# Loading sixteen tiles of a rotary-embedding kernel in 13 transfers in place of 9

## The chip, the cores and the metric

The kernel runs on one core of a Trainium2 chip. The metric is the device time of one execution, in microseconds (us). Kernels that are compared ran in the same rounds on the same chip; a run counts as slow, and stays out of the ratios, when it is over 1.5% above the fastest of its kernel, and all others count as fast. The profile's span (84.2 us) is some 1.8 us shorter than the device time (86.0), since it counts from the program's first to its last recorded instruction.

## The reference

A rotary position embedding in float32, where the last dimension of 64 is split in halves:

```python
# x: (8, 8, 1024, 64); cos_cached, sin_cached: (1024, 32)
out_first  = x_first * cos_cached - x_second * sin_cached
out_second = x_first * sin_cached + x_second * cos_cached
out = concatenate([out_first, out_second], axis=-1)
```

It reads 16.8 MB of x and writes as much, and does only four multiplications and two additions or subtractions for each pair of elements.

## The kernel before

x is cut into 16 tiles of 128 partitions x 2048 numbers (1 MB, 8 KB for each partition). Each tile has its own place on the chip, so no load waits for a store. SyncE issues all loads, the first two tiles singly and the rest in pairs:

```python
xt = []
for first, n in [(0, 1), (1, 1)] + [(c, 2) for c in range(2, n_ch, 2)]:
    t = xp.tile([P, n, F], fp32, name=f"x{first}")
    nc.sync.dma_start(out=t, in_=xf[first:first + n].rearrange("c p m -> p c m"))
    xt += [t[:, i] for i in range(n)]
```

The arithmetic is divided in four ways. Each tile needs two products (with sine and with cosine) and two sums of half size. The scratch tiles `vs` come from a pool of six.

```python
def vector_pool(c, cuts=(0, R)):        # products on VectorE, sums on GpSimd
    s = tv.tile([P, F], fp32, name="vs")             # pool tv: bufs=6
    products(nc.vector, c, s, csp, snp)
    for n0, n1 in zip(cuts, cuts[1:]):
        sums(nc.gpsimd, c, s, n0, n1)
        store(nc.sync, c, n0, n1)
# vector_tensor(c): products on VectorE, sums on TensorE, stored by ScalarE's queue
# on_pool(c):       all on GpSimd, stored by SyncE
def vector_alone(c):                    # all on VectorE
    products(nc.vector, c, acc, csp, snp)
    sums(nc.vector, c, acc, 0, R)
    store(nc.scalar, c)

vector_tensor(0); on_pool(1); vector_pool(2); vector_pool(3); vector_tensor(4)
on_pool(6); vector_pool(5); vector_tensor(7); vector_pool(8); vector_tensor(9)
vector_pool(10); vector_tensor(11); vector_pool(12); vector_pool(13)
vector_pool(14, (0, G, R)); vector_alone(15)
```

SyncE's transfers go through queue q1 and ScalarE's through q10. In the built program the transfers use eight semaphores in turn, so that the issue of a transfer may have to wait until the one eight places before it has landed.

## Time and profile before

| | before |
|---|---|
| device time, median (range) of the first 3 runs | 85.98 us (85.84 to 86.1) |
| span of the profiled run | 84.2 us |
| moved in the span | 33.82 MB, mean 402 GB/s |
| VectorE (DVE) busy | 70.4 us, 84% |
| GpSimd (POOL) busy | 71.4 us, 85% |
| TensorE (PE) / ScalarE (ACT) busy | 40.1 us / 15.7 us |

Two engines are at some 85%, but the DMA engines, read slice by slice, are at nine tenths or more nearly from start to end; the prediction shows those lines. The page's last part tells the two forms of load apart. Its columns are: what is written from what, the issuing queue, the operation and how many, the size of each, and the median time from issue to landing.

```profile
x<-in_x_dram SPq DMA_DIRECT2D x7, 2048.0 KB, 25.0
...
x<-in_x_dram SPq DMA_DIRECT2D x2, 1024.0 KB, 6.3
```

A pair took 25 us from issue to landing although its data alone need 5 us: all loads are issued early and stand in a queue. A long time to landing in this part is a queue, not a slow transfer.

### The profile page before, as it was taken

The page shows a single profiled execution, that of the slowest core. Times are in us where ns is not written, and L with a number is a line of the kernel's source. Part 1 is how long each engine was busy: PE and PEld are TensorE (multiplying, and loading weights), DVE is VectorE, ACT ScalarE, POOL GpSimd, SP SyncE. Part 2 cuts the span into 40 slices and gives each one's busy share as a digit, 9 for nine tenths or more (in the row PEclk, how much of TensorE's full clock was granted, in tenths as well). Part 3 has the DMA queues.
Part 4 walks back from the last instruction along what each step waited for, and adds up shares of the span by engine and source line. Part 5 has one row for each costly group of instructions (what it writes and reads, how often), then busy time and mean ns, then how long its engine had stood idle before and what let it go on. Part 6 is the DMA issues. An engine that isn't in the chain of part 4 may idle for free.

```text
span 84.2 us, 363 instructions
## 1 busy us (share of the span) xinstructions
PE 40.1 (48%) x80; PEld 15.7 (19%) x80; DVE 70.4 (84%) x34; ACT 15.7 (19%) x16; POOL 71.4 (85%) x38
## 2 busy tenths in 40 slices
PE   0000005994930896895949497794949600000000
PEld 0000002422400341423314051332414100000000
DVE  0199997999999999999999982999999999996000
ACT  4399000004040003104040402204040310000000
POOL 3199999999999999999999999999999999970000
PEclk9999999999999569999999999999999999555555
DMA  3899999999999999999999999999999999999991
GB/s 29 282 432 409 420 420 436 417 409 420 436 428 409 417 428 432 432 424 409 421 436 436 432 421 417 424 424 436 432 432 432 413 421 428 428 436 407 432 419 55
DMA packets 4736, 33.82 MB, mean 402 GB/s; under 512 B 448, under 2 KB 448, under 8 KB 768
## 3 DMA queue, kind: packets, MB, share of 16 engines
q1 hardware_dynamic: 3824, 27.40, 78.7%
q10 hardware_dynamic: 912, 6.42, 18.1%
HBM read 17.04 MB, written 16.78 MB: 402 GB/s over the span
## 4 chain that ended last, share of the span: by engine, by line
POOL 53%; DVE 23%; issue 9%; DMA 4%; DVEq 1%; POOLq 0%
POOL x L94 13%; POOL x L93 11%; DVE vs L88 11%; POOL x L89 11%; POOL gs L88 11%; DVE x L89 8%; POOL sn L77 4%; DMA sn<-in_sin_cached_dram 4%; POOL cs L77 3%; DVE acc L88 3%; DVE x L93 1%; DVEq L170 1%; POOLq L93 0%; POOLq L77 0%
## 5 line engine op out<-in xcount | busy, mean ns | idle before, releaser
L119 PE MATMUL acc<-x,plus 128*128 128x512 f32 x40 | 23.3, 666 | 26.4 <-DVE x L89 13.6
L89 DVE TENSOR_TENSOR x<-x,csp 128x2048 f32<-128x2048 f32 x14 | 32.0, 2287 | 0.6
L88 DVE TENSOR_TENSOR vs<-x,snp 128x2048 f32<-128x2048 f32 x13 | 29.7, 2282 | 2.2 <-POOL x L94 1.7
L122 ACT COPY x<-acc 128x1024 f32<-128x1024 f32 x10 | 10.1, 1012 | 49.2 <-PE acc L120 49.2
L94 POOL TENSOR_TENSOR x<-x,vs 128x1024 f32<-128x1024 f32 (+1 forms) x9 | 19.0, 2108 | 0.0
L93 POOL TENSOR_TENSOR x<-x,vs 128x1024 f32<-128x1024 f32 (+1 forms) x9 | 18.9, 2105 | 0.0
L119 PEld LDWEIGHTS acc<-x,plus 128*128 128x128 f32 x40 | 7.5, 208 | 39.4 <-issue 23.9
L120 PE MATMUL acc<-vs,minus 128*128 128x512 f32 x20 | 11.6, 666 | 0.0
L120 PE MATMUL acc<-vs,plus 128*128 128x512 f32 x20 | 10.2, 592 | 0.0
L89 POOL TENSOR_TENSOR x<-x,cs 128x2048 f32<-128x2048 f32 x2 | 9.1, 4546 | 0.2
L88 POOL TENSOR_TENSOR gs<-x,sn 128x2048 f32<-128x2048 f32 x2 | 9.1, 4542 | 0.1
L73 DVE COPY snp<-sn 32x1024 f32<-32x1024 f32 x4 | 4.9, 1223 | 3.9 <-DMA sn<-in_sin_cached_dram 3.8
L120 PEld LDWEIGHTS acc<-vs,minus 128*128 128x128 f32 x20 | 4.4, 219 | 5.9 <-issue 5.9
L77 POOL COPY sn<-sn 32x1024 f32<-32x1024 f32 x3 | 3.1, 1032 | 2.7 <-DMA sn<-in_sin_cached_dram 2.6
L93 POOL TENSOR_TENSOR x<-x,gs 128x1024 f32<-128x1024 f32 x2 | 4.7, 2362 | 0.2
L94 POOL TENSOR_TENSOR x<-x,gs 128x1024 f32<-128x1024 f32 x2 | 4.7, 2357 | 0.0
L120 PEld LDWEIGHTS acc<-vs,plus 128*128 128x128 f32 x20 | 3.8, 190 | 4.8 <-issue 4.8
L74 ACT COPY csp<-cs 32x1024 f32<-32x1024 f32 x4 | 4.0, 1008 | 1.5 <-DMA cs<-in_cos_cached_dram 1.4
L77 POOL COPY cs<-cs 32x1024 f32<-32x1024 f32 x3 | 3.1, 1033 | 0.1
L88 DVE TENSOR_TENSOR acc<-x,snp 128x2048 f32<-128x2048 f32 x1 | 2.3, 2297 | 0.0
L71 ACT ACT_TABLE_LOAD x1 | 1.3, 1283 | 1.2 <-PEq L159 1.2
L93 DVE TENSOR_TENSOR x<-x,acc 128x1024 f32<-128x1024 f32 x1 | 1.2, 1223 | 0.0
(8 smaller groups left out, 2.4 us busy)
## 6 DMA issues: line engine op xcount, KB each, us to landing
x<-in_x_dram SPq DMA_DIRECT2D x7, 2048.0 KB, 25.0
out_dram<-x SPq DMA_DIRECT2D x9, 1024.0 KB, 13.0
out_dram<-x ACTq DMA_DIRECT2D x6, 1024.0 KB, 9.0
x<-in_x_dram SPq DMA_DIRECT2D x2, 1024.0 KB, 6.3
out_dram<-x SPq DMA_DIRECT2D x2, 512.0 KB, 6.0
cs<-in_cos_cached_dram ACTq DMA_DIRECT2D x1, 128.0 KB, 3.4
sn<-in_sin_cached_dram SPq DMA_DIRECT2D x1, 128.0 KB, 3.1
```

The source lines that it names most:

```text
L71: nc.scalar.mul(minus, plus, -1.0)
L73: nc.vector.tensor_copy(out=snp[r * Q:(r + 1) * Q], in_=sn[0:Q])
L74: nc.scalar.copy(out=csp[r * Q:(r + 1) * Q], in_=cs[0:Q])
L77: nc.gpsimd.tensor_copy(out=t[r * Q:(r + 1) * Q], in_=t[0:Q])
L88: eng.tensor_tensor(out=rows(s), in0=xr, in1=tab(stab), op=TT.mult)
L89: eng.tensor_tensor(out=xr, in0=xr, in1=tab(ctab), op=TT.mult)
L93: eng.tensor_tensor(out=xr[:, :, 0], in0=xr[:, :, 0], in1=sr[:, :, 1], op=TT.subtract)
L94: eng.tensor_tensor(out=xr[:, :, 1], in0=xr[:, :, 1], in1=sr[:, :, 0], op=TT.add)
L119: nc.tensor.matmul(a[:, k], plus, xr[:, :, k], start=True, stop=False)
L120: nc.tensor.matmul(a[:, k], plus if k else minus, sr[:, :, 1 - k], start=False, stop=True)
L122: nc.scalar.copy(out=xr, in_=a.rearrange("p k n j -> p n k j"))
L170: with _tile.TileContext(nc) as tc:
```

## The change

The first ten tiles are loaded one by one and the last six in pairs. The intent is that the first tile of each early pair need not wait for the second, so that the engines get their data up to 2.5 us earlier. It costs four more transfers (32 in place of 28).

```diff
-    for first, n in [(0, 1), (1, 1)] + [(c, 2) for c in range(2, n_ch, 2)]:
+    for first, n in [(c, 1) for c in range(10)] + [(c, 2) for c in range(10, n_ch, 2)]:
```

## The prediction

> **What bounds the kernel now.** I read the page's slices first, because they tell in which stretch which resource is full.
>
> ```profile
> DMA  3899999999999999999999999999999999999991
> GB/s 29 282 432 409 420 420 436 417 409 420 436 428 409 417 428 432 432 424 409 421 436 436 432 421 417 424 424 436 432 432 432 413 421 428 428 436 407 432 419 55
> ...
> HBM read 17.04 MB, written 16.78 MB: 402 GB/s over the span
> ```
>
> Each slice is 84.2 / 40 = 2.1 us. From the third slice to the last but one the DMA engines are at nine tenths or more, with no dip, and the rate stays between 407 and 436 GB/s. To see whether "nine tenths" hides idle time, I then asked for the busy time by stretch (columns: engines, granted clock, DMA share, GB/s).
>
> ```profile
> 15.00:25.00 10.00, 7.73 (x15) 2.68 (x13) 9.93 (x5) 2.02 (x2) 9.88 (x4) 1.00 1.01 421
> 35.00:45.00 10.00, 7.79 (x18) 3.04 (x17) 9.93 (x5) 2.02 (x2) 9.84 (x4) 1.00 1.02 428
> 55.00:65.00 10.00, 7.80 (x18) 3.06 (x17) 9.93 (x5) 2.02 (x2) 9.97 (x5) 1.00 1.02 430
> 75.00:82.00 7.00, 0.00 (x0) 0.00 (x0) 2.19 (x2) 0.00 (x0) 0.30 (x1) 0.50 1.01 423
> 82.00:84.20 2.20, 0.00 (x0) 0.00 (x0) 0.00 (x0) 0.00 (x0) 0.00 (x0) 0.50 0.14 60
> ```
>
> The DMA share is 1.0 in all of them, up to 82. The packet records begin at 1.8 us and end at 82.7, so 33.82 MB take 80.9 us, 418 GB/s on average. VectorE (DVE) and GpSimd (POOL) are nearly as full, so the chain of work that ended last has to be read too (start, length, what).
>
> ```profile
> 0.73 3.08 DMA sn<-in_sin_cached_dram
> ...
> 49.65 2.30 POOL x L94
> 51.95 0.02 issue
> 51.98 2.30 DVE vs L88
> ...
> 74.84 1.22 DVE x L93
> 76.06 1.13 DVEq L170
> ```
>
> It starts at the sine table, not at a tile of x. It goes along GpSimd without a gap until 51.95, passes to VectorE, and ends at 77.2. But the span ends at 84.2. What lies between is told by the DMA view of 77 to 84 us:
>
> ```profile
> q1 hardware_dynamic: 321, 1.19, 41.4%
> q10 hardware_dynamic: 144, 1.05, 35.4%
> ...
> out_dram<-x ACTq DMA_DIRECT2D x1, 1024.0 KB, 5.9
> ```
>
> The last store (tile 15, 1.05 MB on q10) is issued at 77.2 and lands 5.9 us later. In that time the engines also move 1.19 MB of earlier stores from q1, together 2.24 MB; at 423 GB/s that is 5.3 us, hence until about 82.5, and the packets do end at 82.7. So the end is set by the queue of bytes, not by the compute chain. The chain even has room: q1's 1.19 MB are 2.8 us of work, and a transfer needs about 1.0 us to its first packet (the tables are issued at 0.73, the first packet is at 1.8), so the last tile could be some 1.5 us later and the engines would still not run dry (my estimate from these numbers).
>
> **What the Trainium skill says.** "DMA: Bandwidth & Descriptors", section "Issuing engines are not separate DMA queues": transfers from all queues run on the same 16 DMA engines. The trace agrees: q1 and q10 together fill a share of 1.0 and never more. Its section "Where 436 GB/s comes from" puts the ceiling at 435 GB/s; the stretches here, at 421 to 430, are within 4% of it, so little rate is left to win. Its section "Why a DMA increments its semaphore by 16 and not by 1" says that each engine taking part ends a transfer with a write to the semaphore; the page counts 448 packets under 512 B, which is 28 transfers x 16. Its section "Measured (HBM→SBUF, 128 partitions, SWDGE, issued from GpSimd)" gives 341 GB/s for 1 MB and 425 for 16 MB, which would speak against smaller transfers; but that is for transfers one at a time, and here they stand in a queue.
>
> **The change part by part.**
>
> *Removed and added.* Four pair loads (tiles 2 to 9) become eight single ones. No byte and no instruction of the computing engines changes; the built program has the same order on each of them. Four more transfers bring 4 x 16 = 64 more semaphore packets. Such packets last 9.4 ns on average in the trace; 64 x 9.4 ns / 16 engines = 0.04 us of engine time.
>
> *Rate of single loads.* The kernel before has both forms next to each other: tile 1 alone is moved at 6.5 to 9.0, then the pair 2 and 3.
>
> ```profile
> 6.50:9.00 2.50, 0.00 (x0) 0.00 (x0) 2.43 (x3) 1.75 (x2) 2.42 (x3) 1.00 1.01 419
> 9.00:11.50 2.50, 0.00 (x0) 0.00 (x0) 2.40 (x2) 0.00 (x0) 2.37 (x3) 1.00 1.02 426
> ```
>
> By the landings tile 1 took 9.03 - 6.48 = 2.55 us and a pair 4.93 to 4.97. If all of the difference were a cost of a transfer c, then b + c = 2.55 and 2b + c = 4.95, so b = 2.40 and c = 0.15, and four more transfers cost 0.6 us. Against it: from 55 to 65 everything that moves is single stores of 1 MB, and the rate there is the highest, 430 GB/s. I choose a cost near zero, and keep 0.6 us as the upper end.
>
> *Moved: arrivals.* A single tile comes every 2.48 us behind tile 1, so tile 2 lands at about 11.5 in place of 13.96, tile 4 at 16.5 in place of 18.9, and so on; the odd tile of each pair comes when it came before. Who waited for these? In the waits by engine x stands once:
>
> ```profile
> DVE vs L88 <- POOL x L94: 1.7, 1, 1.7
> DVE vs L88 <- DMA x<-in_x_dram: 0.4, 1, 0.4
> ```
>
> VectorE is done with tile 0 at 13.55 and starts tile 2 at 13.99: 0.44 us go. From then on it is busy until 50.2, where it waits 1.74 us for a scratch buffer that GpSimd frees at 51.95. GpSimd's work does not start from an x load (it starts tile 1 at 10.44, after its table copies; tile 1 landed at 9.03), so 51.95 stays. The 0.44 us gained turn into a buffer wait of 1.74 + 0.44 = 2.2 us, and VectorE still ends at 77.2.
>
> *Moved: issues on SyncE.* Semaphores for transfers are handed out in a ring of eight in the built program, so a transfer waits for the one eight before it. With more transfers these pairings shift: loads 12-13 and 14-15 now wait for tiles 5 and 6 to land, at 6.48 + 5 x 2.48 = 18.9 and at 21.4. When load 14-15 is issued, tiles 7 to 13 are still queued, seven times 2.5 us. The first store of SyncE (tile 1) waits for tile 8, about 27 in place of 24.33, tile 2's store for tile 0's store to land (34.0) and tile 3's for load 10-11 (36.2). All are behind the loads in q1, whose last one lands at 48.75, so these delays cost nothing. Tile 6's store now waits for tile 4's store, 48.6 in place of 47.4; tiles 1 to 3 (3 MB, 7 us) are queued by then. No later pairing is later than the computing engine, beyond a microsecond for tile 8.
>
> *Sum.* 85.98 + 0.04 (semaphores) + 0 to 0.6 (single form, taken near 0) - 0 (VectorE, swallowed twice: by the buffer wait and by the DMA queue) = 86.0.
>
> **The rivals.** (a) *Earlier data shortens the time.* If VectorE set the end, 0.44 us could go: 85.5. For it: VectorE is on the chain for its last 25 us. Against it: the wait for GpSimd at 51.95 lies between, and the end is the byte queue's. (b) *Each transfer has a price in the queue.* Then 86.6; for it the 2.55 us of tile 1, against it the rate of the stores. (c) *The shifted waits starve the engines*: a store held back on SyncE also holds all behind it, and if q1 and q10 ran empty, that idle time would be added one for one. To reach 2% it would have to be 1.7 us of all engines. By the reckoning above at least 2 MB, 5 us, stand in the queues at each changed wait. Times: 86.5 to 88. (d) *A better mix*: if reads and writes side by side ran faster than reads alone, earlier stores would help; but reads alone run at 421 to 426 and the mix at 423 to 430, and stores do not come earlier. At best 85.7.
>
> **Range and chances.** Runs of the kernel before span 85.84 to 86.1, and the sum is the same time. Rival (a) or (d) gives the low end, 85.5, rival (b) the high end, 86.6. Only (c) leads out of 2%, and I give it 2 in 100; faster by 2% would need the byte queue to move at 434 GB/s or more on average from the first packet to the last, which I give 1 in 100.
>
> **What would show the steps right or wrong.** Right: 512 packets under 512 B; DMA share 1.0 in all stretches from 5 to 82; the wait of VectorE for an x load gone and its wait for GpSimd at 2.2 us; GpSimd's handover still at about 51.95; VectorE's end at about 77.2; the last store landing at about 83.2. Rival (a) shows as an earlier last packet at the same rate and bytes; (b) as a rate of 411 to 419 GB/s between 9 and 24 us, in place of 423 to 426; (c) as a slice of DMA under 9 in the middle, with a SyncE wait for a transfer ending there. The prediction is wrong if the time leaves 85.5 to 86.6, and its mechanism is wrong if the DMA share falls below 1.0 anywhere before the last store.

## The result

The changed kernel took 86.15 us in the median of six runs (85.91 to 86.24), the kernel before 85.97 us (85.79 to 86.1) in the same rounds. The ratio is 1.0016, with a 95% interval of 0.9996 to 1.0036: the same time. Ratios here are the mean time of one kernel's fast runs over that of the other's fast runs of the same rounds, so they are not quite the ratio of the medians quoted.

The page of the changed kernel, its slices, its count of packets and its loads:

```profile
DMA  0999999999999999999999999999999999999991
GB/s 4 307 420 405 424 436 428 393 424 436 432 409 413 397 432 428 436 416 413 424 436 436 428 432 420 416 420 432 436 436 428 432 405 428 424 436 413 434 434 62
DMA packets 4800, 33.82 MB, mean 402 GB/s; under 512 B 512, under 2 KB 512, under 8 KB 832
...
x<-in_x_dram SPq DMA_DIRECT2D x10, 1024.0 KB, 14.3
...
x<-in_x_dram SPq DMA_DIRECT2D x3, 2048.0 KB, 23.3
```

The bytes and the mean rate are those of before, 33.82 MB and 402 GB/s. There are 512 packets under 512 B, 64 more, 16 for each added transfer. The busy time by stretch has no idle DMA either. Its columns are the stretch and its length in us, the busy us and the number of instructions of PE, of its weight loads, of DVE, ACT and POOL, the granted clock of TensorE, the DMA share and GB/s. (A packet counts whole in the stretch in which it starts, so a share can read a little over 1.0.)

```profile
15.00:25.00 10.00, 8.68 (x15) 3.05 (x14) 9.90 (x6) 1.20 (x2) 9.84 (x5) 1.00 1.02 426
35.00:45.00 10.00, 7.80 (x18) 2.87 (x16) 9.93 (x5) 2.02 (x2) 9.84 (x3) 1.00 1.02 430
75.00:82.00 7.00, 0.00 (x0) 0.00 (x0) 2.21 (x2) 0.00 (x0) 0.25 (x1) 0.50 1.01 423
```

Now the waits of VectorE. Before, it waited 0.4 us for x and 1.7 us for GpSimd. In the waits of the changed kernel one line is left:

```profile
DVE vs L88 <- POOL x L94: 2.2, 1, 2.2
```

VectorE starts tile 2 at 13.55 in place of 13.99, and keeps that lead until 49.8. There it waits 2.20 us for the scratch buffer of tile 5, which GpSimd frees at 51.98 in this run and freed at 51.95 in the one before. The chain of work that ended last shows the handover and the end, hardly moved (start, length, what; DVEq is VectorE's instruction queue):

```profile
49.69 2.29 POOL x L94
51.98 0.02 issue
52.00 2.30 DVE vs L88
...
76.08 1.13 DVEq L170
```

The last store, in the DMA view from 77 to 84 us, again finds 1.25 MB of q1 ahead of it and takes 6.0 us, where it took 5.9:

```profile
q1 hardware_dynamic: 329, 1.25, 43.6%
q10 hardware_dynamic: 144, 1.05, 35.4%
...
out_dram<-x ACTq DMA_DIRECT2D x1, 1024.0 KB, 6.0
```

It landed at 83.24, and at 83.16 before (landings of the trace). The issues of SyncE did move. The store of tile 1 went out at 26.54 in place of 24.33, that of tile 2 at 35.46 in place of 28.93, that of tile 3 at 36.55 in place of 34.11. SyncE's waits say for what; first a line of the kernel before, then one of the changed kernel (in total, times, longest):

```profile
SPq L97 <- DMA x<-in_x_dram: 19.0, 3, 8.1
```

```profile
SPq L97 <- DMA out_dram<-x: 20.6, 3, 9.1
```

SyncE now waits 20.6 us for earlier stores, where it waited 5.6. None of it shows in the time, because q1 was still moving loads until 48.8, and the stores stood behind these anyway.

### The profile page after: what moved, and what is told of

Its sections match the earlier page's. It is cut to its first block, busy times and chain, and to the rows that moved or that the text cites. A ratio compares the mean times of both kernels' runs of the same rounds, so it can differ in the third digit from the quotient of the medians.

```text
span 84.2 us, 367 instructions
## 1 busy us (share of the span) xinstructions
PE 39.5 (47%) x80; PEld 15.3 (18%) x80; DVE 70.3 (84%) x34; ACT 15.7 (19%) x16; POOL 71.2 (85%) x38
## 2 busy tenths in 40 slices
DMA packets 4800, 33.82 MB, mean 402 GB/s; under 512 B 512, under 2 KB 512, under 8 KB 832
## 4 chain that ended last, share of the span: by engine, by line
POOL 49%; DVE 23%; issue 14%; DMA 4%; DVEq 1%; POOLq 0%
POOL x L94 12%; DVE vs L88 11%; POOL x L89 11%; POOL gs L88 11%; POOL x L93 9%; DVE x L89 8%; DMA sn<-in_sin_cached_dram 4%; POOL sn L77 4%; POOL cs L77 3%; DVE acc L88 3%; DVE x L93 1%; DVEq L170 1%; POOLq L93 0%; POOLq L77 0%
## 5 line engine op out<-in xcount | busy, mean ns | idle before, releaser
L120 PE MATMUL acc<-vs,minus 128*128 128x512 f32 x20 | 11.1, 639 | 0.0
```

What stands on the lines that cost most here:

```text
L120: nc.tensor.matmul(a[:, k], plus if k else minus, sr[:, :, 1 - k], start=False, stop=True)
```

## The experiments

Theory 1 is the prediction's: the queue of bytes sets the end, and the 0.44 us that VectorE gains go into waits. Theory 2: the chain of computing engines sets the end, with the last store as a fixed tail. Theory 3: the earlier arrival is worth nothing to begin with. Rivals b and c are the prediction's (a price for each transfer; starved DMA engines). Kernels are compared only within the same rounds. An edit is shown against the changed kernel, unless said otherwise.

### Taking away the wait for the scratch buffer

```diff
-    tv = ctx.enter_context(tc.tile_pool(name="tv", bufs=6))
+    tv = ctx.enter_context(tc.tile_pool(name="tv", bufs=7))
```

> The changed kernel with seven scratch buffers for VectorE in place of six, so that the 2.2 us wait for GpSimd at 52 us goes; bytes and transfers are the same. Theory 1 (the end is set by the queue of bytes): VectorE ends at about 75.0 in place of 77.2, the last store is issued about 2.2 us earlier and lands about 2.2 us later after its issue (8.2 us in place of 6.0), the last landing stays at 83.2, the time within 0.3 us of the kernel before (85.7 to 86.3). Theory 2 (the chain of computing engines sets the end): about 84.0, 2 us less.

Measured: 85.83 us against 85.89 of the kernel before, ratio 0.9993 (0.9981 to 1.0006). The wait of VectorE for GpSimd is gone, and VectorE ended 2.6 us earlier, at 74.6 (0.3 us of it because it began earlier in this run). In the DMA view from 74.3 us on, VectorE's last store took nearly all of that back, and GpSimd's last half store (tile 14) took 8.2 us too:

```profile
out_dram<-x ACTq DMA_DIRECT2D x1, 1024.0 KB, 8.1
out_dram<-x SPq DMA_DIRECT2D x1, 512.0 KB, 8.2
```

The half store landed last here, at 83.08, after VectorE's at 82.72. That it was GpSimd's work that held the end is excluded: the half store was issued at 74.91, and in `less_bytes` below, where the queue is short, it lands 2.6 us after its issue. So even the whole wait, five times the gain of the change, is worth nothing that the interval shows. Theory 2, which expected 84.0, falls.

### Taking bytes away, leaving the arithmetic

```diff
         sums(nc.gpsimd, c, s, 0, R)
-        store(nc.sync, c)                      # tiles 1 and 6
 ...
-            store(nc.sync, c, n0, n1)
+            if c not in (2, 3):
+                store(nc.sync, c, n0, n1)
```

> The changed kernel without the stores of tiles 1, 2, 3 and 6 (4.2 MB less of 33.8; the result is wrong on purpose, those rows are never written); the computing engines do the same work. Theory 1 (byte queue): the DMA engines run dry in between and the last store finds a short queue, so it lands about 4 us after its issue in place of 6.0; VectorE still ends at 77.2; time about 84.1 (83.7 to 84.6), 2 us less. Theory 2 (computing chain, with a fixed cost of 5.9 us for the last store): 86.0.

Measured: 84.05 us, ratio 0.9785 (0.9772 to 0.9798), 1.9 us less. The missing rows make the result wrong. VectorE ended at 77.0, 0.2 us from where it ends in the changed kernel. The DMA engines now have idle time (stretches), and the last store takes 3.9 us:

```profile
50.00:60.00 10.00, 7.19 (x16) 2.88 (x16) 8.13 (x4) 1.99 (x2) 10.00 (x5) 1.00 0.65 269
...
75.00:77.00 2.00, 0.00 (x0) 0.00 (x0) 2.00 (x2) 0.00 (x0) 0.06 (x1) 0.50 0.69 277
```

With the same arithmetic the kernel ends 1.9 us sooner as soon as the queue is shorter. Of the 6.0 us that the last store takes in the changed kernel, 3.9 are its own, and 2.1 are the queue before it. That second number should be the room that the computing chain has; the next two runs test it.

### Making the computing chain longer

Products whose values are written again just after were added before the last tile, half of one (`late_half`) or two full ones (`late_two`, whose edit is shown):

```diff
 def vector_alone(c):
+    for _ in range(2):
+        nc.vector.tensor_tensor(out=rows(acc), in0=rows(xt[c]), in1=tab(snp), op=TT.mult)
     products(nc.vector, c, acc, csp, snp)
```

> The changed kernel with one more half multiply of VectorE (1.2 us, its result is overwritten by the same values) before the last tile, so the last store is issued at about 78.4. Theory 1 with the estimate of 1.5 us of room: time unchanged within 0.3 us (85.8 to 86.4). Theory 2: 1.2 us more, 87.2.

> The changed kernel with two more full multiplies of VectorE (2 x 2.3 = 4.6 us) before the last tile, so the last store is issued at about 81.9. Theory 1 with 1.5 us of room: 4.6 - 1.5 = 3.1 us more, about 89.2 (88.7 to 89.8), and a dip in the DMA share before the last store. Theory 2: 4.6 us more, 90.6.

Measured: `late_half` took 86.01 us, ratio 1.0013 (0.9999 to 1.0026); its last store was issued 1.1 us later (78.37 in place of 77.24) and landed in 4.9 us in place of 6.0. `late_two` took 88.51 us, ratio 1.0301 (1.0287 to 1.0315), 2.6 us more. Its stretches at the end show where the queue ran dry:

```profile
75.00:79.00 4.00, 0.00 (x0) 0.00 (x0) 3.97 (x2) 0.00 (x0) 0.14 (x1) 0.50 1.00 415
79.00:81.00 2.00, 0.00 (x0) 0.00 (x0) 1.97 (x3) 0.00 (x0) 0.00 (x0) 0.50 0.40 162
81.00:83.00 2.00, 0.00 (x0) 0.00 (x0) 0.76 (x1) 0.00 (x0) 0.00 (x0) 0.50 0.23 94
```

Of 4.6 us added, 2.6 came out, so 4.6 - 2.6 = 2.0 us were room. This agrees with the 2.1 us above; the prediction's estimate of 1.5 us was too low, and the expectation of 89.2 (88.7 to 89.8) therefore too high, a miss.

### More and fewer transfers

`all_single` loads all sixteen tiles singly (35 transfers), `fours` loads tiles 4 to 15 in fours (25 transfers):

```diff
-    for first, n in [(c, 1) for c in range(10)] + [(c, 2) for c in range(10, n_ch, 2)]:
+    for first, n in [(c, 1) for c in range(n_ch)]:                                          # all_single
+    for first, n in [(0, 1), (1, 1), (2, 2)] + [(c, 4) for c in range(4, n_ch, 4)]:         # fours
```

> All sixteen tiles loaded one by one, 35 transfers. Theory 1 (a transfer costs its bytes, and 16 semaphore packets of 9.4 ns on 16 engines): 86.0, as before. Rival b (0.15 us for each transfer): 7 more than in the kernel before, 1.05 us more, 87.0. Rival c (the ring of eight holds stores back and the engines run dry): over 86.5 with a dip in the DMA share.

> Tiles 4 to 15 loaded in fours, 25 transfers. Tile 4 then lands at about 23.9 in place of 18.9, and VectorE wants it at 23.0, so about 0.9 us of wait, which the buffer wait at 52 us should swallow (1.74 - 0.9 = 0.8 us left). Theory 1: 86.0. Rival b: 3 transfers less, 0.45 us less, 85.5. Theory 2 with arrivals that matter: up to 0.9 us more, 86.9.

Measured: `all_single` 86.2 us, ratio 1.0014 (0.9998 to 1.003); `fours` 86.01 us, ratio 0.9999 (0.9983 to 1.0015). Both shared their rounds with the same runs of the kernel before, so the ten transfers between them are worth 0.0015 x 86 = 0.13 us, 0.013 us for each, inside the noise (the upper end for `all_single`, 1.003, is 0.26 us for seven transfers more, under 0.04 us for each). The stretch from 9 to 24 us, in which all four kernels move nothing but loads, has the same rate in each; in order, the kernel before, the changed kernel, `all_single` and `fours`:

```profile
9.00:24.00 15.00, 9.08 (x16) 3.52 (x16) 14.38 (x7) 1.14 (x2) 14.71 (x6) 1.00 1.02 425
```

```profile
9.00:24.00 15.00, 9.16 (x15) 3.82 (x16) 14.83 (x7) 1.01 (x1) 14.71 (x6) 1.00 1.01 422
```

```profile
9.00:24.00 15.00, 9.51 (x16) 3.81 (x16) 14.83 (x7) 1.01 (x1) 14.72 (x6) 1.00 1.01 423
```

```profile
9.00:24.00 15.00, 9.22 (x15) 3.86 (x16) 13.59 (x7) 1.01 (x1) 14.71 (x6) 1.00 1.01 421
```

The rates of 421 to 425 GB/s follow no order by the size of a transfer. Rival b's 0.15 us per transfer is excluded (it would be 1.05 us for `all_single`), and the profile of `all_single`, with the most loads, has a DMA share of nine tenths or more in every slice between the first two and the last, so rival c falls too. In `fours` VectorE waited 1.2 us for x, and its wait for GpSimd shrank to 0.8 us: the buffer wait swallows a loss as it swallows a gain.

### Is the gain real at all?

Two pairs of twins, each with the loads of before and with those of the change. The lean twins combine the seven buffers with the missing stores of tiles 1, 2, 3 and 6 (the edits above). `lean_pairs` starts from the kernel before, `lean_singles` from the changed one.

> The kernel before (pair loads) with both swallowers taken away: seven scratch buffers, and no stores of tiles 1, 2, 3 and 6 (wrong result on purpose). VectorE waits 0.44 us for tile 2 and then no more, and ends at about 75.4. Theory 1 (the earlier tile is a true gain that the buffer wait and the byte queue swallow): this one is 0.4 us slower than its twin with single loads; both near 82.3. Theory 3 (single loads bring nothing even there, since the two forms cost the same and the tile's arrival does not matter): the two are equal within 0.1 us.

> The changed kernel (single loads) with seven scratch buffers and without the stores of tiles 1, 2, 3 and 6. VectorE has no wait for x and ends at about 75.0. Theory 1: about 0.4 us less than its twin with pair loads, near 81.9. Theory 3: equal to it within 0.1 us.

Measured: 82.99 us (ratio 0.9653, 0.9631 to 0.9674) with pairs and 83.07 us (0.9645, 0.9626 to 0.9665) with single loads: no difference that the intervals would let through (0.07 us, and the half-widths taken together are 0.25 us), and they are 0.7 and 1.2 us above what was expected. By the times alone theory 3 would have won. But the traces show that VectorE did hand over earlier: its last store was issued at 74.97 in place of 75.36, and it no longer was the last to land. The DMA view from 74.7 us on, of the twin with pairs and then of that with single loads:

```profile
out_dram<-x ACTq DMA_DIRECT2D x1, 1024.0 KB, 5.1
out_dram<-x SPq DMA_DIRECT2D x1, 512.0 KB, 4.3
```

```profile
out_dram<-x ACTq DMA_DIRECT2D x1, 1024.0 KB, 4.1
out_dram<-x SPq DMA_DIRECT2D x1, 512.0 KB, 4.8
```

GpSimd's last half store (tile 14, SPq) is issued at 75.3 in both. It and VectorE's last store are together 1.5 MB that move side by side, and in both profiles the one issued second landed last: VectorE's at 80.43 with pairs, GpSimd's at 80.12 with single loads. So VectorE's earlier end met a third thing, which I had left out: GpSimd's own chain. How much of the gain it took is not shown, since the last landings of the two profiled runs are still 0.3 us apart, though the times are not. A second pair of twins has that chain's end gone as well; tile 14 gets neither sums nor a store:

```diff
         products(nc.vector, c, s, csp, snp)
+        if c == 14:
+            return
         for n0, n1 in zip(cuts, cuts[1:]):
```

> The pair-load twin of the lean kernels with the third swallower taken away too: tile 14 is neither summed by GpSimd nor stored (wrong on purpose), so GpSimd ends near 70 and nothing stands in the queue when VectorE's last store is issued at about 75.4. Theory 1: the last store lands about 3.9 us later, at 79.2, 0.4 us after its twin with single loads; time near 81.8. Theory 3: equal to the twin within 0.1 us.

> The single-load twin of the same. Theory 1: the last store is issued at about 75.0 and lands at 78.9; time near 81.4, 0.4 us less than the twin with pairs. Theory 3: equal to it within 0.1 us.

Measured: 82.13 us with pairs (ratio 0.9549, 0.9522 to 0.9577) and 81.59 us with single loads (0.9487, 0.947 to 0.9504). The intervals no longer overlap. The ratios differ by 0.0062, 0.53 us of 86.0. One of the six runs with pairs (83.01, just over 1.5% above the fastest) counts as slow and is not in its ratio; the other five spread from 81.78 to 82.67, which nothing on record explains, and the half-widths of the two intervals (0.0028 and 0.0017) taken together are 0.3 us, so the size is uncertain by that much either way. In the two profiled runs the last store was issued at 75.17 and 74.84 and landed at 79.03 and 78.71, with 3.9 us in both, 0.3 us apart. The wait of the twin with pairs is the one that the change removes:

```profile
DVE vs L88 <- DMA x<-in_x_dram: 0.4, 1, 0.4
```

Theory 3 falls: the earlier tile is worth about what the wait says, within that uncertainty, in a kernel where neither the scratch buffers, nor the queue of bytes, nor GpSimd's chain can take it back.

### Letting the DMA engines stand idle

A control for theory 1: the loads of x begin later, because the first one has to wait for a small copy of VectorE out of the sine table.

```diff
     t = xp.tile([P, n, F], fp32, name=f"x{first}")
+    if first == 0:
+        nc.vector.tensor_copy(out=t[0:Q, 0, 0:1], in_=sn[0:Q, 0:1])
```

> The changed kernel with the first load of x held back until the sine table has landed and VectorE has copied 32 numbers of it into the tile (overwritten by the load), so that x starts about 2.9 us later and the DMA engines stand idle that long. The arithmetic stays right. Theory 1: the idle time of the engines is added in full, 88.9 (88.4 to 89.4). Theory 2: only what GpSimd loses by tile 1, which lands at 12.0 where GpSimd wants it at 10.4, 1.5 us, so 87.5.

Measured: 88.76 us, ratio 1.0319 (1.0305 to 1.0333), 2.7 us more than the kernel before. The first stretches show the gap:

```profile
3.00:4.00 1.00, 0.00 (x0) 0.00 (x0) 0.26 (x2) 0.01 (x1) 0.15 (x1) 1.00 0.01 0
...
24.00:34.00 10.00, 6.15 (x14) 2.31 (x13) 9.93 (x5) 2.02 (x2) 10.00 (x5) 1.00 1.00 398
```

The first tile landed at 8.72, 2.1 us after that of the changed kernel (6.59), not 2.9 us as I had reckoned. The last store landed at 85.69, 2.45 us later. The computing chain lost only 0.9 us (VectorE's last store was issued at 78.13 in place of 77.24), so theory 2 falls here again. Of the 2.45 us, 2.1 are the idle engines at the start. The rest fits the slower stretch from 24 to 34, with 398 GB/s where the changed kernel has 420; 22 GB/s less over 10 us is 0.22 MB, or 0.5 us. That this slow stretch is not a consequence of the edit is likely but not shown (see the last section).

No version tried that gives the right result beats both kernels by more than their spread; `seven_buffers`, at 0.9993, is not told apart from the kernel before.

## Why the prediction was right

The time (86.0 predicted, 86.15 measured) and the mechanism held.

- *The bound.* Bytes set the end: less bytes with the same arithmetic took 1.9 us off, less waiting in the arithmetic with the same bytes took nothing off, and idle DMA engines came out in the time.
- *Removed and added.* 64 more packets, as reckoned, and the price of a transfer is near zero; from 25 to 35 transfers the time stays within 0.2 us (ratios 0.9999 to 1.0016).
- *The single form.* The choice to take its cost as near 0, against tile 1's 2.55 us, was right. Tiles 2 to 7 of the changed kernel landed 2.45 to 2.49 us apart, which is what half of a pair's 4.95 us is.
- *Arrivals.* VectorE's 0.44 us turned into a buffer wait of 2.2 us, as predicted (measured 2.20), and GpSimd's handover stayed. The prediction named two swallowers of the gain. It missed a third, GpSimd's last half store, which is issued within some 2 us of VectorE's and which lands last in `seven_buffers` and in the lean twin with single loads.
- *Issues on SyncE.* The stores of tiles 1 to 3 moved to about where they were put, and cost nothing. One step was off: tile 6's store was to be held until 48.6 by tile 4's; it went out at 47.41, since tile 4's store was itself issued 1.9 us earlier (36.85 in place of 38.79) and had landed at 46.02.
- *The room of the chain.* Estimated at 1.5 us, it measured 2.0 (`late_two`) and 2.1 (own time of a store, 3.9 us, against 6.0). The prediction's own figures, 2.8 us of queued bytes less 1.0 us to the first packet, give 1.8 us, nearer to it than the 1.5 it wrote.
- *Two readings that do not hold.* A gain of 2% is 1.7 us, and 33.82 MB in 80.9 - 1.7 = 79.2 us are 427 GB/s, not the 434 that the prediction names as the rate needed; its own stretches reach 430, so that gain was less far off in rate than it said. And the share of q1 and q10 together is not "never more" than 1.0: its stretches read up to 1.02, through the way packets are counted. The forecast rested on neither.

## What to carry to other kernels

Where the DMA share is 1.0 nearly from the first packet to the last, as here, finer loads only changed who waits: ask of an earlier arrival which wait comes next on that engine, and then what stands in the queue when its last store is issued. The own time of a lone transfer against its time at the end of the kernel tells how much room the arithmetic has. If an experiment that removes the known obstacles still shows no gain, look which transfer lands last in it before calling the gain unreal; here the store of a third engine had come to land last.

## What the Trainium skill lacked or had wrong

- The Trainium skill's page "DMA: Bandwidth & Descriptors", section "Where 436 GB/s comes from", says that for transfers between HBM and SBUF the HBM side, some 358 GB/s, binds. The sentence lacks a condition that its section "Measured (HBM→SBUF, 128 partitions, SWDGE, issued from GpSimd)" gives, that both cores which share an HBM domain stream. Here, with the kernel on one core, 421 to 430 GB/s moved in the stretches of 10 us and more with a full DMA share that are shown (398 in the slow one of the last point, and 413 in one of the changed kernel that is not shown, from 25 to 35 us), reading alone, writing alone and both; the ceiling of 435 GB/s in the same section is the one that fits.
- The same page, section "Measured (HBM→SBUF, 128 partitions, SWDGE, issued from GpSimd)", gives rates by size and does not compare sizes for loads that stand in a queue (nor does it say that its own ran one at a time; that is the prediction's reading). Queued, 1 MB, 2 MB and 4 MB loads ran alike, at 421 to 425 GB/s, and a transfer more cost about 0.01 us, which is inside the noise.
- No page that I read gives the time of a lone 1 MB store of SyncE or ScalarE from issue to landing; it was 3.9 us in `less_bytes`, `late_two` and both bare twins.
- On no page, and not explained by these runs: in 8 of the 13 profiles one slice of about 2 us between 27 and 31 us runs at 310 to 371 GB/s, with the DMA share still at nine tenths or more (in `late_half` 319 GB/s; in the kernel before and the changed one no slice there is below 397). It costs up to 0.6 us of DMA time (my estimate: 425 less 310 GB/s over 2.2 us) and comes with no one form of load. What it is stays open.
